# Gate and up products of a split-fp32 SwiGLU: one 512-column matmul for the weight's high part, a PSUM bank per side, product and low part on GpSimd

## The chip, the core and the metric

The kernel runs on one core of a Trainium2 chip. The time is the device time of one execution in microseconds. Beside it stands one profiled execution of the same kernel, whose trace names every instruction, its engine, its source line and its tiles. Engines are PE (TensorE), DVE (VectorE), ACT (ScalarE), POOL (GpSimd) and SP, which issues most of the DMAs.

## The reference

A two-layer decoder trunk for 256 tokens with `D_MODEL = 1024`. Each layer is a half-step SwiGLU, a token mixer and another half-step SwiGLU, each behind an RMSNorm with shift, scale and gate from the conditioning vector `c`. Layer 0 mixes with block-sparse attention (MoBA), layer 1 with MLA. All is float32. The change touches the four SwiGLUs, `D_FF = 2816`:

```python
def swiglu(h, w_gate, w_up, w_down):
    return (jax.nn.silu(h @ w_gate) * (h @ w_up)) @ w_down

for layer in range(DEPTH):
    mods = c_act @ ada_w[layer] + ada_b[layer]
    ...
    h = modulate(rms_norm(x, norm_g[layer, 0]), sh1, sc1)
    x = x + 0.5 * g1[:, None, :] * swiglu(h, ffn_w_gate[layer, 0], ffn_w_up[layer, 0], ffn_w_down[layer, 0])
    ...  # the token mixer, then the second swiglu
```

## The kernel before

**Split operands.** Every large product is made of float32r parts: a value is held as a high part (rounded) and a low part (the rest), and a product is three matmuls, high by high, high by low and low by high, summed in PSUM. `mm3` issues them (lines 394 to 396 of the profile) and then books their time on the planner's clock with `pe`. Weights come by DMA into a raw tile (`wload`); `split` makes of it `hi` on ACT and `lo` on DVE, in tiles of 128x1024, from rings of eight each (`splitp`). `in_turn` issues both, so both have line 196. `nextw` keeps one weight load ahead of the one in use.

**The activations.** `new_h` makes two tiles, `hh` and `hl`, high and low part of the transposed normalised input, each [128, 2 token blocks, 1024]. `hk_both` gives the slice of 128 features k of both token blocks, 256 columns.

**One FFN** (`ffn`) has three stages. The first 512 features of `D_FF` are made with tokens on the partitions, 512 columns a matmul. The other 2304 are made in nine blocks of 256, each two steps f of 128 features. In one step the weight is the stationary operand: for gate and then up, eight k by one `mm3` of 256 columns, 48 matmuls, all into one PSUM bank whose halves are gate and up. Then ACT makes silu of the gate half (line 560), DVE multiplies it by the up half (line 561), ACT rounds that to `gh` and DVE makes `gl`, its low part (`split_evac`, line 196). The last stage multiplies `gh` and `gl` by the down weights, 512 columns a matmul.

**Other work in the queues.** Shift, scale and gate need `c_act @ ada_w`. That is done on DVE, a multiply-add of 128x1024 for each of the 128-row pieces of `ada_w` (`ada_vec`, line 211), and the pieces are spread over an FFN by the planner: whenever its clock passes the next due time (`ada_pace`, 172 us of booked time for an FFN's pieces, 90 in the last), one piece and its DMA are issued. The first FFN also carries the bias tables for the attention (`bias_steps`, lines 722 and 785), in part on DVE, PE and POOL. Engines work off their instructions in order; the order within each is fixed when the kernel is built.

Of the kernel before, what the change touches and what calls it, by code (L numbers as in the profile page):

```python
# [10 lines left out]
F32 = mybir.dt.float32  # L11
F32R = mybir.dt.float32r
BF16 = mybir.dt.bfloat16
I32 = mybir.dt.int32
AF = mybir.ActivationFunctionType
ALU = mybir.AluOpType
# [4 lines left out]
P = 128  # L21
D = 1024
KD = D // P
S = 256
NT = S // P
# [62 lines left out]
def trunk(ctx: ExitStack, tc: tile.TileContext, a: dict, out: bass.AP):  # L88
    nc = tc.nc
# [5 lines left out]
    hp = ctx.enter_context(tc.tile_pool(name="hp", bufs=1))  # L95
# [8 lines left out]
    def nm(s):  # L104
        uid[0] += 1
        return f"{s}_{uid[0]}"
# [13 lines left out]
    def run_next():  # L120
        assert pend
        was, busy[0] = busy[0], True
        pend.pop(0)[2]()
        busy[0] = was

    def until(cond):
        while not cond():
            run_next()

    def pe(us):  # L130
        clock[0] += us
        if busy[0]:
            return
        while pend and pend[0][0] <= clock[0]:
            run_next()
        while pace[0] and clock[0] >= pace[1]:
            pace[1] += pace[0]
            ada(1)
# [54 lines left out]
    def in_turn(fn, *args, on="p", **kw):  # L193

        if started:
            return fn(*args, **kw)  # L196
        with behind(on):
            chain[on] = fn(*args, **kw)  # L198
        return chain[on]
# [94 lines left out]
    def ada(n):  # L294
        for _ in range(n):
            if next(ada_it, "end") != "end":
                ada_done[0] += 1

    def ada_pace(vectors, us):

        n = vectors * KD - ada_done[0]
        pace[0] = us / n if n > 0 else None
        pace[1] = clock[0] + (us / n if n > 0 else 0.0)
# [89 lines left out]
    def mm3(ps, lh, ll, rh, rl, start, stop):  # L393
        nc.tensor.matmul(ps, lh, rh, start=start, stop=False)  # L394
        nc.tensor.matmul(ps, lh, rl, start=False, stop=False)  # L395
        nc.tensor.matmul(ps, ll, rh, start=False, stop=stop)  # L396
        pe(3 * max(256, rh.shape[-1]) * 0.422e-3)

    def mm_tile():
        return ps_mm.tile([P, 512], F32, tag="mm", name=nm("mm"))  # L400

# [6 lines left out]
    def split_evac(hi, lo, ps):  # L408
        in_turn(nc.scalar.activation, hi, ps, AF.Copy, on="a")
        return in_turn(nc.vector.tensor_tensor, lo, ps, hi.bitcast(F32), op=ALU.subtract, on="v")  # L410
# [60 lines left out]
    pair = []  # L471

    def new_h(t):
        if t == 0:
            pair[:] = [hp.tile([P, NT, D], F32R, tag=g, name=nm(g)) for g in ("hh", "hl")]
        return pair[0][:, t, :], pair[1][:, t, :], set(), list(pair)

    def hk(h, k):
# [1 line left out]
        return kslice(h[0], k), kslice(h[1], k)  # L480

    def hk_both(h, k):
        for t in range(NT):
            until(lambda: k in h[t][2])
        return [x[:, :, k * P:(k + 1) * P] for x in h[0][3]]

    def norm_T(t, key, keep=None):
        h = new_h(t)
# [17 lines left out]
    def ffn(layer, idx, h, after, ada_to, start=None):  # L506

        last = (layer, idx) == (1, 1)
        with ExitStack() as st:
            gp = st.enter_context(tc.tile_pool(name=nm("gp"), bufs=1))  # L510
            gT = {}
            accs = start() if start else {t: [] for t in range(NT)}
            ada_pace(ada_to, 90.0 if last else FFN_PACE)
            parts = [] if start else [[], []]
            for t in range(NT):
                for i, pl in enumerate(parts):
                    ps = mm_tile()
                    for k in range(KD):
                        if len(pl) <= k:
                            pl += nextw()  # L520
                        mm3(ps, *hk(h[t], k), *pl[k], start=k == 0, stop=k == KD - 1)
                    accs[t].append(ps)
                acc = accs.pop(t)
                g = gp.tile([P, FB], F32, tag="g", name=nm("g"), bufs=2)
                nc.scalar.activation(g, acc[0], AF.Silu)
                nc.vector.tensor_tensor(g, acc[1], g, op=ALU.mult)

                def fin(t=t, g=g):
                    pt = tr_tile()
                    for j in range(FB // P):  # L530
                        nc.tensor.transpose(kslice(pt, j), kslice(g, j), ident)
                    pe(FB // P * 0.11)
                    gh, gl = [gp.tile([P, FB], F32R, tag=f"{nme}_{t}", name=nm(nme)) for nme in ("gh", "gl")]
                    split_evac(gh, gl, pt)
                    for j in range(FB // P):
                        gT[j, t] = (kslice(gh, j), kslice(gl, j))
                later(G_WAIT, fin)
            gq = gp
            for f0 in range(FB, F, S):
                if f0 == SIDE_TO * S:  # L540
                    while start and next(side[0], "end") != "end":
                        bias_step()
                    gq = st.enter_context(tc.tile_pool(name=nm("gp"), bufs=1))
                if start and f0 == ROPE_AT * S:
                    with behind("v", "a", "g"):
                        rope_tables()
                        mla_consts()
                parts = [[], []]
                for f in range(f0 // P, (f0 + S) // P):
                    ps = mm_tile().rearrange("p (i t q) -> p i t q", i=2, q=P)  # L550
                    for i, pl in enumerate(parts):
                        for k in range(KD):
                            if len(pl) <= k:
                                pl += nextw()
                            mm3(ps[:, i], *[w[:, f * P - f0:(f + 1) * P - f0] for w in pl[k]],
                                *hk_both(h, k), start=k == 0, stop=k == KD - 1)
                            if start and k in HOOKS and f0 < SIDE_TO * S:
                                bias_step()
                    g = gp.tile([P, NT, P], F32, tag="gT", name=nm("g"), bufs=2)
                    nc.scalar.activation(g, ps[:, 0], AF.Silu)  # L560
                    nc.vector.tensor_tensor(g, ps[:, 1], g, op=ALU.mult)  # L561
                    gh, gl = [gq.tile([P, NT, P], F32R, tag=f"{nme}{f}", name=nm(nme)) for nme in ("gh", "gl")]
                    split_evac(gh, gl, g)
                    for t in range(NT):
                        gT[f, t] = gh[:, t, :], gl[:, t, :]
            for half in range(2):
                acc = [mm_tile() for _ in range(NT)]
                wl = []

                def mms(t, k):  # L570
                    until(lambda: (k, t) in gT)
                    mm3(acc[t], *gT[k, t], *wl[k], start=k == 0, stop=k == KF - 1)

                lag = LAG if half == 1 else 0
                for k in range(KF):
                    if len(wl) <= k:
                        wl += nextw()
                    mms(0, k)
                    if k - lag >= 0:
                        mms(1, k - lag)  # L580
                gate = mod((layer, 2 * idx), "g")
                resid(0, half, acc[0], gate, last)
                if half == 1:
                    ada_until(ada_to)
                    after(0)
                    for k in range(KF - lag, KF):
                        mms(1, k)
                resid(1, half, acc[1], gate, last)
            after(1)
# [4 lines left out]
    def attention(ap, g, qTs, kTs, vs, bias, oT, state, after_s=None):  # L594
# [63 lines left out]
        def av():  # L658
            until(lambda: state.get("v", 0) > g)
            po = at_tile().rearrange("p (r t q) -> p r t q", r=GH // 2, t=NT)  # L660
            for pr in range(GH // 2):
                for t in range(NT):
                    for i in range(2):
                        e = 2 * pr + i
                        for kb in range(t + 1):
                            nc.tensor.matmul(po[i * DH:(i + 1) * DH, pr, t, :], vs(e, kb),  # L666
                                             pT[t, e, kb], start=kb == 0, stop=kb == t)
            pe(2.4)
            kk = g * (GH // 2)
            pov = po.rearrange("p r t q -> p t r q")  # L670
            hi, lo = [x[:, :, kk * P:(kk + 2) * P].rearrange("p t (r q) -> p t r q", q=P) for x in oT[0][3]]
            split_evac(hi, lo, pov)
            for t in range(NT):
                oT[t][2].update((kk, kk + 1))
            state["av"] = g + 1
# [609 lines left out]
```

## Time and profile before

| What | Value |
|---|---|
| median of 3 runs | 1064.85 us (1064.45 to 1068.0) |
| the profiled execution's own time | 1067.16 us |
| its span in the profile | 1065.4 us |
| busy share PE, DVE, ACT, POOL | 96%, 76%, 54%, 7% |
| mean granted TensorE clock | 0.998 |
| steps f in the gate and up stages | 72 (18 in each FFN) |
| gate and up matmuls of 256 columns | 3456 (1152 on each of lines 394, 395, 396) |

PE's busy share counts the time between a matmul's start and its modelled end, and these overlap; the pace is read from the starts. A group's row has the group's line, engine, operation, tiles and shapes, its count, then its busy time and the mean ns of one, and at last the idle time of its engine just before it with what ended that.

### The profile page before, as it was taken

The numbers are of one execution on the slowest core, as the hardware profiler recorded it, in microseconds if no ns is written. First come the engines' busy times: TensorE is split into PE (matmuls) and PEld (weight loads), VectorE is DVE, ScalarE is ACT, GpSimd is POOL, SyncE is SP. The second block draws the span as 40 slices with busy tenths as digits, with TensorE's granted clock in tenths as the row PEclk, the third lists the DMA queues.
The fourth block names the chain that finished last, engine by engine and source line by source line (L and its number), as shares of the span: only waits on it lengthen the run. The fifth ranks groups of instructions, "written<-read, shape, count | busy, mean of one in ns | idle before, by whom it ended". The sixth has DMA issues, their size and how long they took to land.

```text
span 1065.4 us, 17278 instructions
## 1 busy us (share of the span) xinstructions
PE 1020.8 (96%) x6663; PEld 899.3 (84%) x6663; DVE 810.9 (76%) x1244; ACT 578.6 (54%) x1048; POOL 70.1 (7%) x119
## 2 busy tenths in 40 slices
PE   4999999998999999999999999999988899999998
PEld 2499999886778789999887999988766778999986
DVE  5999977886875789889688888867778758755642
ACT  4364545357675765545348544533868777545531
POOL 4001000002121000000000000000043200000000
PEclk9999999999999999999999999999999999999999
DMA  9999987996845479989897997986354337665450
GB/s 311 322 304 287 376 288 278 335 318 206 310 162 170 139 236 345 337 293 332 295 313 227 328 329 251 318 303 205 117 162 142 119 119 236 223 204 187 161 177 20
DMA packets 166934, 260.65 MB, mean 245 GB/s; under 512 B 8030, under 2 KB 110214, under 8 KB 166852
## 3 DMA queue, kind: packets, MB, share of 16 engines
q1 hardware_dynamic: 164496, 254.70, 70.3%
q0 software_dynamic: 976, 3.37, 1.0%
q10 hardware_dynamic: 1380, 1.49, 0.5%
q8 instruction: 52, 0.85, 0.3%
q14 instruction: 30, 0.25, 0.1%
HBM read 255.33 MB, written 4.19 MB: 244 GB/s over the span
## 4 chain that ended last, share of the span: by engine, by line
PE 77%; DVE 10%; ACT 4%; DMA 4%; POOL 3%; issue 3%; SPq 0%; DVEq 0%; ACTq 0%; POOLq 0%
PE mm L394 23%; PE mm L396 23%; PE mm L395 23%; DVE lo L196 3%; POOL hr L703 3%; DMA adaw<-in_ada_w_dram 2%; PE mm L198 2%; ACT hi L196 1%; DVE oh L722 1%; PE adaps L222 1%; PE at L666 1%; PE at L611 1%; DVE acc L211 1%; DMA raw<-in_ffn_w_gate_dram 1%; ACT y L196 1%
## 5 line engine op out<-in xcount | busy, mean ns | idle before, releaser
L196 DVE TENSOR_TENSOR lo<-raw,hi 128x1024 fp32r<-128x1024 f32 (+2 forms) x316 | 374.3, 1199 | 80.2 <-ACT hi L196 79.3
L196 ACT ACTIVATE hi<-raw 128x1024 fp32r<-128x1024 f32 (+2 forms) x316 | 324.1, 1040 | 171.5 <-PE mm L396 103.6
L394 PE MATMUL mm<-hh,hi 128*128 128x256 f32 x1152 | 328.6, 285 | 0.0
L396 PE MATMUL mm<-hh,lo 128*128 128x256 f32 x1152 | 326.7, 284 | 0.5 <-DVE lo L196 0.5
L395 PE MATMUL mm<-hl,hi 128*128 128x256 f32 x1152 | 326.5, 283 | 0.0
L395 PEld LDWEIGHTS mm<-hl,hi 128*128 128x128 f32 x1152 | 221.7, 192 | 0.6 <-issue 0.2
L396 PEld LDWEIGHTS mm<-hh,lo 128*128 128x128 f32 x1152 | 221.6, 192 | 0.7 <-DVE lo L196 0.7
L394 PEld LDWEIGHTS mm<-hh,hi 128*128 128x128 f32 x1152 | 221.7, 192 | 0.6 <-issue 0.2
L211 DVE SCALAR_TENSOR_TENSOR acc<-adaw,cact,acc 128x1024 f32<-128x1024 f32 x126 | 162.8, 1292 | 20.6 <-DMA adaw<-in_ada_w_dram 16.2
L394 PE MATMUL mm<-hi,gh 128*128 128x512 f32 x352 | 138.0, 392 | 0.0
L395 PE MATMUL mm<-lo,gh 128*128 128x512 f32 x352 | 137.0, 389 | 0.0
L396 PE MATMUL mm<-hi,gl 128*128 128x512 f32 x352 | 137.0, 389 | 0.0
L394 PE MATMUL mm<-hi,hh 128*128 128x512 f32 (+1 forms) x240 | 96.7, 404 | 5.0 <-ACT hh L196 5.0
L396 PE MATMUL mm<-hi,hl 128*128 128x512 f32 (+1 forms) x240 | 94.0, 392 | 1.5 <-DVE hl L196 1.4
L395 PE MATMUL mm<-lo,hh 128*128 128x512 f32 (+1 forms) x240 | 93.4, 390 | 0.0
L560 ACT ACTIVATE g<-mm 128x256 f32<-128x256 f32 x72 | 27.3, 379 | 94.5 <-PE mm L396 94.5
L396 PEld LDWEIGHTS mm<-hi,gl 128*128 128x128 f32 x352 | 66.1, 188 | 13.8
L394 PEld LDWEIGHTS mm<-hi,gh 128*128 128x128 f32 x352 | 66.1, 188 | 13.2
L395 PEld LDWEIGHTS mm<-lo,gh 128*128 128x128 f32 x352 | 66.1, 188 | 13.1
L196 ACT ACTIVATE gh<-g 128x256 fp32r<-128x256 f32 x72 | 29.9, 416 | 69.6 <-DVE g L561 69.6
L394 PEld LDWEIGHTS mm<-hi,hh 128*128 128x128 f32 x240 | 45.1, 188 | 16.1 <-ACT hh L196 7.8
L396 PEld LDWEIGHTS mm<-hi,hl 128*128 128x128 f32 x240 | 45.1, 188 | 13.2 <-DVE hl L196 4.5
(222 smaller groups left out, 1114.8 us busy)
## 6 DMA issues: line engine op xcount, KB each, us to landing
adaw<-in_ada_w_dram SPq DMA_DIRECT2D x144, 512.0 KB, 6.8
raw<-in_ffn_w_gate_dram SPq DMA_DIRECT2D x42, 1024.0 KB, 7.3
raw<-in_ffn_w_up_dram SPq DMA_DIRECT2D x42, 1024.0 KB, 6.9
raw<-in_ffn_w_down_dram SPq DMA_DIRECT2D x40, 1024.0 KB, 6.6
raw<-in_moba_w_qkv_dram SPq DMA_DIRECT2D x16, 512.0 KB, 5.0
adaw<-in_kv_ada_w_dram SPq DMA_DIRECT2D x16, 512.0 KB, 5.6
raw<-in_ffn_w_down_dram SPq DMA_DIRECT2D x8, 512.0 KB, 3.6
raw<-in_moba_w_qkv_dram SPq DMA_DIRECT2D x4, 1024.0 KB
```

The source lines that it names most:

```text
L196: return fn(*args, **kw)
L198: chain[on] = fn(*args, **kw)
L211: nc.vector.scalar_tensor_tensor(acc, wt, cact[:, k:k + 1], bz if k == 0 else acc, op0=ALU.mult, op1=ALU.add)
L222: nc.tensor.transpose(kslice(pt, j), kslice(acc, 4 * hh + j), ident)
L394: nc.tensor.matmul(ps, lh, rh, start=start, stop=False)
L395: nc.tensor.matmul(ps, lh, rl, start=False, stop=False)
L396: nc.tensor.matmul(ps, ll, rh, start=False, stop=stop)
L560: nc.scalar.activation(g, ps[:, 0], AF.Silu)
L611: nc.tensor.matmul(ps3[:, i, :], qTs(e, t), kTs(e, nk), start=bias is not None, stop=bias is not None or i == len(es) - 1)
L666: nc.tensor.matmul(po[i * DH:(i + 1) * DH, pr, t, :], vs(e, kb), pT[t, e, kb], start=kb == 0, stop=kb == t)
L703: nc.gpsimd.tensor_tensor(r, v2, mhalf[:, :nh], op=ALU.pow)
L722: return fn(*args, **kw)
```

## The change

`hh` and `hl` become one tile of [128, 2 parts, 2 token blocks, 1024], and `hk_both` hands out the slice of both parts, 512 columns. `mm2` takes the place of `mm3` in the nine blocks: the weight's high part meets both parts of h in one matmul of 512 columns, whose result fills a whole bank (high by high in the first half, high by low in the second), and the weight's low part meets the high part of h in one of 256 columns, added to the second half. Gate and up have a bank each. After each side ACT copies the second half to SBUF and DVE adds the first half to it. Then ACT makes silu in SBUF, GpSimd the product, ACT `gh`, and GpSimd `gl`. A step has 32 matmuls in place of 48. The planner books 346.6 ns for an `mm2`, where it booked 324.1 ns for an `mm3`.

```diff
+    def mm2(ps, wh, wl, both, start, stop):
+        nc.tensor.matmul(ps, wh, both, start=start, stop=False)
+        nc.tensor.matmul(ps[:, 1], wl, both[:, 0], start=False, stop=stop)
+        pe(1e-3 * (6 * P / 2.4 + 2 * 13.3))
...
     def new_h(t):
         if t == 0:
-            pair[:] = [hp.tile([P, NT, D], F32R, tag=g, name=nm(g)) for g in ("hh", "hl")]
+            both = hp.tile([P, 2, NT, D], F32R, tag="hh", name=nm("hh"))
+            pair[:] = [both[:, 0], both[:, 1], both]
...
-        return [x[:, :, k * P:(k + 1) * P] for x in h[0][3]]
+        return h[0][3][2][:, :, :, k * P:(k + 1) * P]
...
                 for f in range(f0 // P, (f0 + S) // P):
-                    ps = mm_tile().rearrange("p (i t q) -> p i t q", i=2, q=P)
+                    sides = gp.tile([P, 2, NT, P], F32, tag="g", name=nm("g"), bufs=2)
                     for i, pl in enumerate(parts):
+                        ps = mm_tile().rearrange("p (i t q) -> p i t q", i=2, q=P)
                         for k in range(KD):
                             if len(pl) <= k:
                                 pl += nextw()
-                            mm3(ps[:, i], *[w[:, f * P - f0:(f + 1) * P - f0] for w in pl[k]],
-                                *hk_both(h, k), start=k == 0, stop=k == KD - 1)
+                            mm2(ps, *[w[:, f * P - f0:(f + 1) * P - f0] for w in pl[k]],
+                                hk_both(h, k), start=k == 0, stop=k == KD - 1)
...
-                    g = gp.tile([P, NT, P], F32, tag="gT", name=nm("g"), bufs=2)
-                    nc.scalar.activation(g, ps[:, 0], AF.Silu)
-                    nc.vector.tensor_tensor(g, ps[:, 1], g, op=ALU.mult)
+                        sd = sides[:, i]
+                        nc.scalar.activation(sd, ps[:, 1], AF.Copy)
+                        nc.vector.tensor_tensor(sd, ps[:, 0], sd, op=ALU.add)
+                    g = sides[:, 0]
+                    nc.scalar.activation(g, g, AF.Silu)
+                    nc.gpsimd.tensor_tensor(g, g, sides[:, 1], op=ALU.mult)
...
-                    split_evac(gh, gl, g)
+                    nc.scalar.activation(gh, g, AF.Copy)
+                    nc.gpsimd.tensor_tensor(gl, g, gh.bitcast(F32), op=ALU.subtract)
```

More of the change, by code (lines that the diff above doesn't have):

```diff
@@ L670, in av @@
             pov = po.rearrange("p r t q -> p t r q")
-            hi, lo = [x[:, :, kk * P:(kk + 2) * P].rearrange("p t (r q) -> p t r q", q=P) for x in oT[0][3]]
+            hi, lo = [x[:, :, kk * P:(kk + 2) * P].rearrange("p t (r q) -> p t r q", q=P) for x in oT[0][3][:2]]
             split_evac(hi, lo, pov)
```

## The prediction

> **What bounds the kernel now.** First I read the page's totals, then the busy time by stretch inside the four gate and up stages (the second FFN, the third, the fourth, and the end of the first). The columns are PE, PEld, DVE, ACT, POOL, granted clock, DMA share, GB/s.
>
> ```profile
> PE 1020.8 (96%) x6663; PEld 899.3 (84%) x6663; DVE 810.9 (76%) x1244; ACT 578.6 (54%) x1048; POOL 70.1 (7%) x119
> 405.00:491.00 86.00, 86.00 (x721) 86.00 (x720) 76.22 (x90) 41.40 (x59) 0.00 (x0) 1.00 0.93 319
> 597.00:681.00 84.00, 84.00 (x700) 83.83 (x700) 69.75 (x83) 39.94 (x58) 0.00 (x0) 1.00 0.87 302
> 906.00:990.00 84.00, 84.00 (x699) 83.83 (x698) 51.93 (x63) 43.20 (x62) 0.00 (x0) 1.00 0.58 193
> 117.00:165.00 48.00, 48.00 (x404) 48.00 (x403) 41.32 (x56) 24.39 (x36) 0.00 (x0) 1.00 0.94 327
> ```
>
> In these stretches PE never pauses; DVE is at 89%, 83%, 62% and 86%, ACT at about half, POOL at nothing. The chain that ended last shows one exception: from about 51 to 91 us, in the first FFN, it runs through DVE, as here.
>
> ```profile
> 51.06 1.21 DVE lo L196
> ...
> 82.16 1.27 DVE acc L211
> 83.43 1.13 DVE lo L196
> 84.56 1.57 DVE oh L722 x8
> ...
> 89.56 1.14 DVE lo L196
> ```
>
> The silus of line 560 by stretch (ACT's busy time and count) show that about four steps f fall into it:
>
> ```profile
> 50.00:75.00 25.00, 0.79 (x2) 1.00 0.91 300
> 75.00:100.00 25.00, 0.85 (x2) 0.93 0.88 287
> ```
>
> So gate and up are PE's, but for some 40 us and four steps that are DVE's, where the bias tables are made. PE's pace is read from starts of matmuls, three apart:
>
> ```profile
> 475.47 0.28 PE L394 MATMUL mm<-hh,hi 128*128 128x256 f32 x1
> 475.83 0.28 PE L394 MATMUL mm<-hh,hi 128*128 128x256 f32 x1
> 777.59 0.33 PE L394 MATMUL mm<-hi,qlT 128*128 128x384 f32 x1
> 778.11 0.33 PE L394 MATMUL mm<-hi,qlT 128*128 128x384 f32 x1
> 514.76 0.39 PE L394 MATMUL mm<-hi,gh 128*128 128x512 f32 x1
> 515.44 0.39 PE L394 MATMUL mm<-hi,gh 128*128 128x512 f32 x1
> L394 PE MATMUL mm<-hh,hi 128*128 128x256 f32 x1152 | 328.6, 285 | 0.0
> ```
>
> A matmul of 256 columns takes 0.120 us, one of 384 0.173, one of 512 0.227: a straight line, 0.107 us for 256 columns and about 13.3 ns for each matmul whatever its width. A step f of 48 matmuls takes 5.76 us, a block 11.52, the nine blocks of an FFN 103.7.
>
> How much cover DVE and ACT have is seen in the ring of split tiles. The first `lo` below ends at 385.7 and is first read by PE at 392.12, at the start of the second FFN's blocks: 6.4 us ahead. Later ACT waits for a slot that PE frees; the tile whose `lo` ends at 461.53 is first read at 475.83 (quoted above), 14.3 us ahead (tiles paired by their place in the order).
>
> ```profile
> 384.47 2.35 DVE L196 TENSOR_TENSOR lo<-raw,hi 128x1024 fp32r<-128x1024 f32 x2
> 392.12 0.28 PE L394 MATMUL mm<-hh,hi 128*128 128x256 f32 x1
> 460.30 1.23 DVE L196 TENSOR_TENSOR lo<-raw,hi 128x1024 fp32r<-128x1024 f32 x1 [0.60 <-ACT hi L196]
> 460.65 1.06 ACT L196 ACTIVATE hi<-raw 128x1024 fp32r<-128x1024 f32 x1 [0.38 <-PE mm L395]
> ```
>
> So a stage starts with about 6 us in hand: DVE or ACT may fall short by that much over 18 steps, 0.36 us a step, before PE waits.
>
> **PE, what it gains.** A pair of 512 and 256 columns takes 0.227 + 0.120 = 0.347 us in place of 0.360. There are 72 x 16 = 1152 pairs: 1152 x 13.3 ns = 15.4 us, 3.84 in each FFN; a step becomes 5.55 us. The columns streamed stay the same (768 a pair). The new matmul reads its columns in four runs of 128; the one of 256 reads two such runs and lies on the same line as the others, so I add nothing for that. [...]
>
> **DVE, what stays and what grows.** DVE loses the product and `gl` and gets two additions of the same shape, so nothing by count. The rows of the second FFN's stretch:
>
> ```profile
> L196 DVE TENSOR_TENSOR lo<-raw,hi 128x1024 fp32r<-128x1024 f32 x32 | 38.3, 1220 | 2.7 <-ACT hi L196 2.7
> L211 DVE SCALAR_TENSOR_TENSOR acc<-adaw,cact,acc 128x1024 f32<-128x1024 f32 x20 | 25.6, 1278 | 1.7 <-DMA adaw<-in_ada_w_dram 1.6
> L561 DVE TENSOR_TENSOR g<-mm,g 128x256 f32<-128x256 f32 x15 | 6.3, 419 | 2.6 <-ACT g L560 2.6
> ```
>
> The planner now books 22.5 ns more a pair, so `ada` pieces (and their DMAs on SP's queue) come earlier: 0.72 us a block more on its clock, or 0.2 piece a block where 48 are paced over 172 us; over this stretch of 7.47 blocks 1.9 us of DVE. The DMA share rises from 0.93 by the same few per cent and stays under 1.
>
> The unknown is what GpSimd does to DVE. Trace of before, while the bias tables are masked:
>
> ```profile
> 77.99 2.06 POOL L785 TENSOR_SCALAR_AFFINE_SELECT bt<-bt 128x2048 f32<-128x2048 f32 x1 [55.97 <-ACT bt L722]
> 95.04 3.23 POOL L785 TENSOR_SCALAR_AFFINE_SELECT bt<-bt 128x2048 f32<-128x2048 f32 x1 [14.99 <-DMA adaw<-in_ada_w_dram]
> 95.18 1.22 DVE L196 TENSOR_TENSOR lo<-raw,hi 128x1024 fp32r<-128x1024 f32 x1
> 96.32 3.02 DVE L211 SCALAR_TENSOR_TENSOR acc<-adaw,cact,acc 128x1024 f32<-128x1024 f32 x1
> ```
>
> The same POOL operation took 2.06 alone and 3.23 beside a DVE `lo` that ended at 96.40: it waited 1.17. The DVE multiply-add behind it took 3.02 in place of 1.28: it could start its work only at 99.34 - 1.28 = 98.06, so POOL held it for 1.66 us of its own 2.06. Whoever starts first stops the other. [...] Which DVE operations are stopped I take likewise from the rows: `lo` and `acc`, 67 of 86 us, 0.8.
>
> No row has a GpSimd operation of this shape. The nearest:
>
> ```profile
> L429 POOL TENSOR_TENSOR rstd<-var,mhalf 128x1 f32<-128x1 f32 x10 | 5.6, 556 | 585.1 <-DVE var L427 585.1
> 331.02 1.66 POOL L703 TENSOR_TENSOR hr<-hv,mhalf 128x8 f32<-128x8 f32 x1 [13.99 <-DVE hv L702]
> masks.py:199 POOL TENSOR_SCALAR_AFFINE_SELECT ident<-ident 128x128 f32<-128x128 f32 x1 | 0.3, 312 | 0.1
> ```
>
> The select grows from 0.31 us at 128 elements to 2.06 at 2048, 0.91 ns each; 256 elements of one operand would be 0.43, the low end. The two-operand power goes from 0.556 at one column to 1.66 at eight, 0.40 us fixed; 1.66 is the high end. I take 0.40 + 2 x 256 x 0.91 ns = 0.87 us, as it is an operation of two operands with a cheap function. [...] Its hold on DVE is 0.4 less, as with the select: 0.47, between 0.03 and 1.25. Four such a block, on DVE's path 0.8 of the time: 1.5 us a block.
>
> Second FFN: the 86 us are 7.47 blocks, which PE now does in 82.8. DVE needs 76.2 + 1.9 + 7.47 x 1.5 = 89.3: 6.5 short, 7.8 over nine blocks, 6.4 of it in hand. Loss 1.4. Third: 69.75 + 1.5 + 7.29 x 1.5 = 82.2 in 80.9; in hand. Fourth: no shortage. First: in the four steps that are DVE's, eight holds of 0.47 x 0.8 add 3.0 us and PE gains nothing; the other 14 steps gain 14 x 0.213 = 3.0.
>
> **ACT, which now waits more.** Its rows:
>
> ```profile
> L560 ACT ACTIVATE g<-mm 128x256 f32<-128x256 f32 x72 | 27.3, 379 | 94.5 <-PE mm L396 94.5
> L196 ACT ACTIVATE gh<-g 128x256 fp32r<-128x256 f32 x72 | 29.9, 416 | 69.6 <-DVE g L561 69.6
> ACT gh L196 <- DVE g L561: 9.1, 10, 2.8
> ACT hi L196 <- PE mm L395: 6.4, 13, 0.9
> ```
>
> A step now costs it two `hi` (2 x 1.06), two copies and a silu (3 x 0.38) and `gh` (0.42): 3.68 us. Behind the copy waits silu, for DVE's addition: 0.91 each time nothing lies between, as `gh` waits for the product now (9.1 us in 10). `gh` waits for the addition and then for POOL: 0.91 + 0.87 + about 0.8 in which POOL waits for the DVE operation that just began = 2.6. What is queued behind it is the next `hi`, and DVE's `lo` waits for that. In the built order about half of the silus and half of the `gh`s have a `hi` between: 0.45 + 1.9 on average, 6.0 us a step. PE's 5.55 plus 0.36 in hand is 5.9, so ACT costs another 0.1 x 18 = 1.8 us in each of the two FFNs where DVE is full; in the fourth the waits are shorter and cost nothing.
>
> Banks are no limit: four in the ring and one a side of 2.77 us leave 8.3 us to empty one. `gl` late is hidden, too: the down stage reads the last step's tile after 21 others.
>
> **The sum.** First FFN 0; second -3.84 + 1.4 + 1.8 = -0.6; third -3.84 + 1.8 = -2.0; fourth -3.84. Together -6.4 us: 1067.2 becomes 1060.8 for the profiled execution, which lies 2.3 over the median; on the median's scale 1058.5. About 0.3%, 3.2 us, can be told from no change.
>
> **Rivals.** *DVE becomes the bound.* If the POOL operation takes 1.3 us, its hold is 0.9, or 2.9 us a block. The second FFN is then 20 us short over its nine blocks, 6.4 of it in hand, and ends 13.9 - 3.84 = 10 later; the third, 14 short, 3.7 later; the first 5.8 - 3.0 = 2.8 later; the fourth still gains 3.84. Together +12.7, 1077.5 on the median's scale; with an operation of 1.66, by the same steps, over 1100. It decides from about 1.05 us on, where the sum is 0. For it: DVE at 89%, and the power at 1.66. Against: most of that row is the power. Chance 0.32. *ACT's waits eat the gain*: from 6.1 us a step (5.76 + 0.36) on, a stage is no faster than before; at 6.15 in the middle FFNs the sum is about 0, 1065. For it: the estimate of 6.0; against: `hi` could be put between. Chance 0.11. [...] Chance 0.04. The forecast, with everything from the full 15.4 to 3.3 gained, has 0.53.
>
> **How the numbers follow.** Full gain gives 1049, the low end. The upper end, 1082, takes in the DVE rival up to an operation of about 1.4 us. Faster is the forecast, 0.53; same the two small rivals, 0.15; slower the DVE rival, 0.32. The forecast's own range is 1049 to 1061.6.
>
> **What would show it.** Right: PE starts 0.347 us a pair; POOL operations of 0.9 when alone and up to 2.1 beside DVE; `lo` and `acc` with single ones stretched by about 0.5; the lead of `lo` over PE shrinking through the second FFN and lasting through the fourth; the fourth FFN's stage about 3.8 us shorter. Wrong: a pair at 0.360; PE waiting for `lo` or `hi` by more than a few us in all; POOL operations of over 1.1 alone.

## The result and the profile after

The changed kernel takes 1092.29 us (median of 4 runs, 1091.56 to 1094.3) against 1065.17 of the kernel before on the same chip: a ratio of 1.0253, 95% interval 1.0229 to 1.0276. It is slower by 27 us where 6 us faster was forecast, and 10 us beyond the range. The profiled execution took 1092.67 us, its span is 1090.5.

From the page of the changed kernel: the totals, the granted clock in 40 slices of 27 us, and the groups of the new tail; behind them the clock's row of the kernel before.

```profile
PE 1027.2 (94%) x5511; PEld 846.5 (78%) x5511; DVE 837.4 (77%) x1244; ACT 613.5 (56%) x1192; POOL 243.5 (22%) x263
PEclk9999999999999999989998999999899999999999
...
L402 PE MATMUL mm<-hh,hi 128*128 128x512 f32 x1152 | 412.5, 402 | 3.5 <-DVE g L571 3.5
...
L574 POOL TENSOR_TENSOR g<-g 128x256 f32<-128x256 f32 x72 | 96.9, 1345 | 367.5 <-DVE g L571 364.1
...
L576 ACT ACTIVATE gh<-g 128x256 fp32r<-128x256 f32 x72 | 30.1, 418 | 140.4 <-POOL g L574 136.3
L577 POOL TENSOR_TENSOR gl<-g,gh 128x256 fp32r<-128x256 f32 x72 | 76.1, 1056 | 39.5 <-ACT gh L576 39.5
L571 DVE TENSOR_TENSOR g<-mm,g 128x256 f32<-128x256 f32 x144 | 59.7, 415 | 31.4 <-ACT g L570 22.0
```

```profile
PEclk9999999999999999999999999999999999999999
```

Four things are seen. PE has 1152 matmuls fewer, yet its busy time rose. The clock row has three slices at 8, where before all were at 9. GpSimd's product takes 1.345 us on average. ACT waits 136.3 us for it ahead of `gh`, where before it waited 69.6 us for DVE. PE's direct wait on the new tail is only 3.5 us (bank release after an addition); so most of the 27 us is not waiting at that point.

Where, is worked out from the starts of the first and the last matmul of each FFN's nine blocks (lines 394 and 396 before, 402 and 403 after). Differences to before, in us of span:

| | nine blocks of FFN 1, 2, 3, 4 | all that lies between, from start to end | sum |
|---|---|---|---|
| after | +5.5, +4.4, -0.5, -1.9 | +17.8 | +25.2 |

The four stages that the prediction reckoned with lost 7 us; 18 us were lost where no instruction had been edited, above all from the end of the second FFN's blocks to the start of the third's (+5.4) and from the end of the third's to the start of the fourth's (+8.9).

The saving on PE itself is there, in the fourth FFN. Timeline of the changed kernel, PE:

```profile
939.84 0.28 PE L403 MATMUL mm<-hh,lo 128*128 128x256 f32 x1
939.96 0.40 PE L402 MATMUL mm<-hh,hi 128*128 128x512 f32 x1
940.19 0.28 PE L403 MATMUL mm<-hh,lo 128*128 128x256 f32 x1
...
941.60 0.28 PE L403 MATMUL mm<-hh,lo 128*128 128x256 f32 x1
```

Five pairs in 1.76 us are 0.352 us a pair; forecast 0.347, before 0.360. The 256-column matmul starts 0.23 to 0.24 us after the one of 512, not 0.227.

### The profile page after: what moved, and what is told of

Read it like the earlier page. It is cut to its first block, busy times and chain, and to the rows that moved or that the text cites. A ratio compares the mean times of both kernels' runs of the same rounds, so it can differ in the third digit from the quotient of the medians.

```text
span 1090.5 us, 15304 instructions
## 1 busy us (share of the span) xinstructions
PE 1027.2 (94%) x5511; PEld 846.5 (78%) x5511; DVE 837.4 (77%) x1244; ACT 613.5 (56%) x1192; POOL 243.5 (22%) x263
## 5 line engine op out<-in xcount | busy, mean ns | idle before, releaser
L196 DVE TENSOR_TENSOR lo<-raw,hi 128x1024 fp32r<-128x1024 f32 (+2 forms) x316 | 389.3, 1248 | 91.5 <-ACT hi L196 91.1
L402 PE MATMUL mm<-hh,hi 128*128 128x512 f32 x1152 | 412.5, 402 | 3.5 <-DVE g L571 3.5
L402 PEld LDWEIGHTS mm<-hh,hi 128*128 128x128 f32 x1152 | 217.8, 189 | 57.1 <-DVE g L571 5.3
L574 POOL TENSOR_TENSOR g<-g 128x256 f32<-128x256 f32 x72 | 96.9, 1345 | 367.5 <-DVE g L571 364.1
L211 DVE SCALAR_TENSOR_TENSOR acc<-adaw,cact,acc 128x1024 f32<-128x1024 f32 x126 | 170.4, 1353 | 8.6 <-DMA adaw<-in_ada_w_dram 7.9
L576 ACT ACTIVATE gh<-g 128x256 fp32r<-128x256 f32 x72 | 30.1, 418 | 140.4 <-POOL g L574 136.3
L394 PE MATMUL mm<-hi,hh 128*128 128x512 f32 (+1 forms) x240 | 100.1, 418 | 7.8 <-ACT hh L196 7.8
L396 PE MATMUL mm<-hi,hh 128*128 128x512 f32 (+1 forms) x240 | 96.0, 400 | 1.2 <-DVE hh L196 1.1
L577 POOL TENSOR_TENSOR gl<-g,gh 128x256 fp32r<-128x256 f32 x72 | 76.1, 1056 | 39.5 <-ACT gh L576 39.5
L571 DVE TENSOR_TENSOR g<-mm,g 128x256 f32<-128x256 f32 x144 | 59.7, 415 | 31.4 <-ACT g L570 22.0
L570 ACT ACTIVATE g<-mm 128x256 f32<-128x256 f32 x144 | 53.4, 372 | 20.8 <-PE mm L403 20.0
```

The source lines that it names most:

```text
L211: nc.vector.scalar_tensor_tensor(acc, wt, cact[:, k:k + 1], bz if k == 0 else acc, op0=ALU.mult, op1=ALU.add)
L402: nc.tensor.matmul(ps, wh, both, start=start, stop=False)
L570: nc.scalar.activation(sd, ps[:, 1], AF.Copy)
L571: nc.vector.tensor_tensor(sd, ps[:, 0], sd, op=ALU.add)
L574: nc.gpsimd.tensor_tensor(g, g, sides[:, 1], op=ALU.mult)
L576: nc.scalar.activation(gh, g, AF.Copy)
```

## Experiments

The theories at first: GpSimd's *hold* on DVE; the *chain* or queue, in which ACT's `gh`, and behind it `hi`, `lo`, the copies and the additions, wait for GpSimd; the *banks*. A later one, from the 18 us outside the stages: the *booking* of the pair on the planner's clock. Ratios are to the kernel before on the same chip, with 95% intervals; its median was 1064.5 to 1066.1 us in the four sets of runs.

**1. Product and low part on DVE.** GpSimd has no part in the tail.

```diff
-                    nc.gpsimd.tensor_tensor(g, g, sides[:, 1], op=ALU.mult)
+                    nc.vector.tensor_tensor(g, g, sides[:, 1], op=ALU.mult)
...
-                    nc.gpsimd.tensor_tensor(gl, g, gh.bitcast(F32), op=ALU.subtract)
+                    nc.vector.tensor_tensor(gl, g, gh.bitcast(F32), op=ALU.subtract)
```

> The changed kernel with product and low part on DVE in place of GpSimd; matmuls, banks, copies and additions stay. Queue theory (ACT stands at gh for GpSimd, hi and lo come late behind it, PE stalls and its clock is cut): the waits of gh fall from 136 us to about 60, and the time to 1058-1066, although DVE has two operations a step more. Hold theory (GpSimd's holds on DVE's lo and acc are the cost): the holds of 23 us go, DVE gets 60 us more work, 1065-1080. Bank and addition theory (two banks a step, the copy and addition are the cost, whoever does the rest): no gain, 1085 or more.

1083.66 us, 1.0171 [1.0131, 1.0212], in the gap between the answers of the hold and of the banks. Without GpSimd two thirds of the loss are still there.

**2. Only the tail on GpSimd.** The kernel before, its three matmuls and one bank for both sides; ACT copies the up half to SBUF, GpSimd does product and `gl`.

> The kernel before with only the tail of the change: its three matmuls a pair and one bank a step stay, ACT copies the up half to SBUF, GpSimd makes product and low part, and DVE loses both. Queue theory: gh waits for GpSimd by some 2 us a step as in the changed kernel, hi and lo come late, 1075-1090. Hold theory: DVE loses 60 us of work and gets some 20 us of holds, so 1060-1067. Bank and addition theory: the tail alone costs nothing, 1063-1067.

1070.12 us, 1.005 [1.0036, 1.0065], again none of the three answers. GpSimd's work alone, at 5 us, doesn't make the 27.

**3. `gh` on GpSimd too**, so that ACT waits for nothing there.

```diff
-                    nc.scalar.activation(gh, g, AF.Copy)
+                    nc.gpsimd.tensor_copy(gh, g)
```

> The changed kernel with the rounding copy gh on GpSimd too, so ACT never waits for GpSimd, while GpSimd has three operations a step and holds DVE more often. Queue theory: ACT's waits at gh are gone, 1058-1070. Hold theory: half as many holds again, 1095-1110. Bank and addition theory: 1085-1095.

1081.12 us, 1.0164 [1.0116, 1.0212]: 9 to 11 us better than the change (by the ratios, by the medians), though GpSimd does a third operation and the `lo` and `acc` of DVE take 14 us longer still. In its trace the group of line 402 has no idle time before it, so PE's wait for a bank is gone too. No answer fits: ACT's wait for GpSimd has a price, but is not the bulk of the 27.

**4. Product on DVE, only `gl` on GpSimd.**

> The changed kernel with the product on DVE and only the low part gl on GpSimd: ACT waits at gh for a DVE operation again, as in the kernel before, and one GpSimd operation a step of two still holds DVE. Queue theory: nearly all comes back, 1055-1066. Hold theory: half of the loss stays, 1072-1080. Bank and addition theory: 1085 or more.

1076.05 us, 1.0104 [1.0071, 1.0138]: the product's place is worth 16 us. This is in the range of the hold's answer, but by chance: what stays of the loss is the booking's, as 7 and 13 show. In this run's trace the four stages gain 3.7 us together (+1.8, -1.0, -2.6, -1.9), and the time between them loses 13.0. That is the loss that no theory so far explained, and it led to the booking: an FFN books 288 pairs x 22.5 ns = 6.5 us more, while the `ada` pieces stay paced over 172 us.

**5. The change with the old booking.**

```diff
-        pe(1e-3 * (6 * P / 2.4 + 2 * 13.3))
+        pe(3 * 256 * 0.422e-3)
```

> The changed kernel, whose pair of matmuls is booked on the planner's clock at 324.1 ns again, as the three matmuls were, in place of 346.6; nothing else differs. Booking theory: an FFN books 6.5 us more in the changed kernel (288 pairs of 22.5 ns), while the pace of 172 us for the ada pieces stays, so pieces fall past the end of gate and up and stand ahead of the next norm on DVE and on SP's queue; with the old booking the 13 to 16 us outside gate and up go, and with them most of the clock lost at the transitions after the second and third FFN: 1076 to 1080 us. Bank and GpSimd theory: the waits lie in gate and up and what follows them, the planner's order hardly matters: 1088 to 1093 us.

1075.32 us, 1.0094 [1.0065, 1.0124], the booking answer to within 1 us: 17 us back, by a number that no engine ever sees.

**6. The kernel before with the new booking.**

```diff
-        pe(3 * max(256, rh.shape[-1]) * 0.422e-3)
+        pe(3 * max(256, rh.shape[-1]) * 0.422e-3 if len(rh.shape) == 2 else 1e-3 * (6 * P / 2.4 + 2 * 13.3))
```

> The kernel before, in which only the booking of the three matmuls of gate and up is raised from 324.1 to 346.6 ns; the instructions are the same, in another order. Booking theory: the transitions after the second and third FFN get later by 4 to 8 us each, 1073 to 1080 us. Bank and GpSimd theory: without the split sides nothing waits, 1064 to 1066 us.

1081.37 us, 1.0149 [1.0104, 1.0194], the booking answer and 1 us more. The same instructions in another order cost 15 us.

**7. Product on DVE and the old booking** (4 and 5 together).

> The changed kernel with the product on DVE, only the low part on GpSimd (1076.05 us with the new booking), and the old booking of 324.1 ns. Booking theory: the 13 us outside gate and up go, the saving of 8 ns a pair stays: 1060 to 1063 us. The other theory: 1073 to 1077 us, as with the new booking.

1060.38 us, 0.9954 [0.9934, 0.9973]: faster than both kernels. Its four stages gain 1.5, 2.3, 2.6 and 2.4 us.

**8. As 7, with the 512 columns in one run**: the tile of both parts is laid out by slices of 128 features.

```diff
-            both = hp.tile([P, 2, NT, D], F32R, tag="hh", name=nm("hh"))
+            both = hp.tile([P, KD, 2, NT, P], F32R, tag="hh", name=nm("hh"))
```

> As the run with the product on DVE and the old booking, but both parts of h lie one behind the other for each slice of 128 features, so that the 512 columns of the moving operand are one contiguous run in place of four of 128. If the four runs cost time, the 512-column matmul starts its successor after 227 ns in place of 235, a pair takes 347 ns in place of 352, and the time falls by a further 4 to 6 us (1056 where the other gives 1061). If they don't, 352 stays and the times agree within 1 us.

1059.58 us, 0.9941 [0.992, 0.9962], not to be told from 7. In its timeline the 256-column matmul still starts 0.23 to 0.24 us after the one of 512, so the four runs of 128 aren't what makes the pair longer than 0.347:

```profile
899.67 0.40 PE L402 MATMUL mm<-hh,hi 128*128 128x512 f32 x1
899.91 0.28 PE L403 MATMUL mm<-hh,lo 128*128 128x256 f32 x1
```

**9. As 4 (new booking), `FFN_PACE` 178.5 in place of 172.**

> The changed kernel with the product on DVE and the new booking of 346.6 ns a pair (1076.05 us as it was), in which only FFN_PACE is raised from 172 to 178.5, by the 6.5 us that an FFN books more. If the ada pieces past the end are what the booking costs, their number by the end of the second FFN is 98 again and the time is 1058 to 1064 us. If the booking acts through the due times of other work instead, it stays at 1073 to 1077 us.

1067.6 us, 1.002 [1.0006, 1.0035]: half of the 16 us came back. Neither answer fits by itself, so pieces and due times had to be parted (13, 14).

**10. As 7, with a dummy product on GpSimd** behind DVE's; nobody reads its result.

```diff
+                    dm = gp.tile([P, NT, P], F32, tag="dm", name=nm("dm"), bufs=1)
+                    nc.gpsimd.tensor_tensor(dm, g, sides[:, 1], op=ALU.mult)
```

> The run with the product on DVE, the low part on GpSimd and the old booking (1060.4 us), with 72 further GpSimd products of 128x256 behind DVE's, whose result nobody reads. Hold theory: that GpSimd stops DVE while it works is what the product on GpSimd costs (1075.3 with it, the old booking in both): 1070 to 1076 us. Chain theory: it is that the high part on ACT, and behind it the copies, the additions and the banks, wait for GpSimd's product; nobody waits for the dummy, so 1060 to 1064 us.

1072.41 us, 1.0068 [1.0051, 1.0085]: 12 us for work that nobody waits for. So the hold is shown, and cost that much here, beside a DVE that in 7 is busy for 81.01 of 84 us of the second FFN's stage (405 to 489). It doesn't divide the 15 us between 5 and 7 into hold and chain: here DVE still makes the product itself, 31 us of work that it does not have in 5, and run 3, which takes ACT out of the chain, gained 9 to 11 though the hold grew. The two overlap, and how much of the 15 is whose stays open. The groups on DVE show the hold, first in 7, then here:

```profile
L196 DVE TENSOR_TENSOR lo<-raw,hi 128x1024 fp32r<-128x1024 f32 (+2 forms) x316 | 384.3, 1229 | 74.3 <-ACT hi L196 73.6
...
L211 DVE SCALAR_TENSOR_TENSOR acc<-adaw,cact,acc 128x1024 f32<-128x1024 f32 x126 | 165.0, 1309 | 6.8 <-DMA adaw<-in_ada_w_dram 5.5
```

```profile
L196 DVE TENSOR_TENSOR lo<-raw,hi 128x1024 fp32r<-128x1024 f32 (+2 forms) x316 | 397.8, 1273 | 67.4 <-ACT hi L196 66.8
...
L211 DVE SCALAR_TENSOR_TENSOR acc<-adaw,cact,acc 128x1024 f32<-128x1024 f32 x126 | 168.4, 1337 | 6.2 <-DMA adaw<-in_ada_w_dram 5.3
```

The same `lo` and `acc` take 13.5 and 3.4 us longer, 17 in all, 0.23 for each dummy.

**11. As 1 (all on DVE), with the old booking.**

> The changed kernel with product and low part on DVE (1083.66 us with the new booking) and the old booking; GpSimd has no part. If a low part on GpSimd is no more than a hold on DVE, this gives 1056 to 1060 us, as fast as the run with it on GpSimd or faster. If DVE is full in the first two FFNs, which gets 30 us more, it gives 1065 to 1072 us.

1065.33 us, 0.9997 [0.998, 1.0014]: 18 us better than 1 by the booking, and 5 behind 7. `gl` on GpSimd holds DVE as well, but takes 72 operations off it: in the profile of this run `lo` and `acc` have 374.6 and 163.0 us, 11.7 less than in 7, and DVE's own `gl` 30.3.

**12. As 5, with five banks for matmul tiles and three for transposes.**

```diff
-    ps_mm = ctx.enter_context(tc.tile_pool(name="ps_mm", bufs=4, space=PSUM))
-    ps_tr = ctx.enter_context(tc.tile_pool(name="ps_tr", bufs=4, space=PSUM))
+    ps_mm = ctx.enter_context(tc.tile_pool(name="ps_mm", bufs=5, space=PSUM))
+    ps_tr = ctx.enter_context(tc.tile_pool(name="ps_tr", bufs=3, space=PSUM))
```

> The changed kernel with the old booking (1075.3 us), with five PSUM banks in the ring of the matmul tiles in place of four, and three in place of four for the transposes. If the ring is the limit in gate and up, the 6.7 us in which PE waits there for DVE's addition go and it gives 1066 to 1070 us. If the waits only move to the next thing that is late (the high part, lo), it stays at 1073 to 1077 us; the ring of three could cost some us in the attention stages.

1072.87 us, 1.0061 [1.004, 1.0081]. The group of line 402, first with four banks, then with five:

```profile
L402 PE MATMUL mm<-hh,hi 128*128 128x512 f32 x1152 | 411.6, 401 | 6.8 <-DVE g L571 6.7
```

```profile
L402 PE MATMUL mm<-hh,hi 128*128 128x512 f32 x1152 | 411.7, 401 | 0.2
```

The 6.7 us of waiting for a bank are gone, the time falls by 2.4, with overlapping intervals, to just under the second answer. In the traces the four stages are 5.2 us shorter than in 5, and the stretch from the first FFN's blocks to the second's, with the MoBA attention, is 6.2 longer. Whether that is the ring of three or the clock, which falls there twice in this trace, was not parted; the same stretch is 4.1 longer than before in 10, with four banks in each ring. So the banks have a share in what the stages lose, and what a fifth is worth alone stays open.

**13. Two clocks.** As 4: due times by the new booking, the pace of the pieces by a second clock with the old one.

```diff
-    def pe(us):
-        clock[0] += us
+    def pe(us, us_p=None):
+        clock[0] += us
+        clock_p[0] += us if us_p is None else us_p
...
-        while pace[0] and clock[0] >= pace[1]:
+        while pace[0] and clock_p[0] >= pace[1]:
```

> The changed kernel with the product on DVE; the planner has two clocks: due times run by the new booking of 346.6 ns a pair, the pace of the ada pieces by a second clock with the old 324.1. If the booking costs by the pieces alone, this is the 1060.4 us of the old booking (1058 to 1062). If it costs by the due times, 1076 stays; if by both in halves, as the raised pace left it, 1065 to 1069 us.

1060.91 us, 0.9961 [0.9944, 0.9977]. All of the 16 us come back: the due times of the other work cost nothing here.

**14. The kernel before, `FFN_PACE` 165.5 in place of 172.**

> The kernel before, in which only FFN_PACE is cut from 172 to 165.5, so that the ada pieces come earlier by the 6.5 us an FFN that the new booking moved them, and nothing else is booked otherwise. If the pieces are the cost: 1076 to 1082 us, as with the new booking in the kernel before (1081.4). If the due times are: 1064 to 1067 us.

1080.04 us, 1.0142 [1.0111, 1.0172], as in 6. The pieces are the whole cost of the booking. Counted in the traces, DVE has done 96 pieces ahead of the last residuals of the second FFN in the kernel before and in 5, 7 and 13: twelve vectors of eight, what is due there. In the change and in 1, 3, 4, 6 and 14 it has done 98; at the third FFN 137 where 136 are due. The trace shows what that does, at the end of the second FFN. DVE in the kernel before, then here (the residual is `ry` and `x`, then the norm's `var`; `acc<-adaw,cact,bz` opens the next vector):

```profile
554.81 0.68 DVE L495 TENSOR_TENSOR ry<-mm,gate 128x512 f32<-128x512 f32 x1
555.53 0.69 DVE L496 TENSOR_TENSOR x<-x,ry 128x512 f32<-128x512 f32 x1
...
557.53 0.15 DVE L427 SCALAR_TENSOR_TENSOR var<-ssq,ssq 128x1 f32<-128x1 f32 x1
```

```profile
552.12 1.28 DVE L211 SCALAR_TENSOR_TENSOR acc<-adaw,cact,bz 128x1024 f32<-128x1024 f32 x1
...
555.46 1.28 DVE L211 SCALAR_TENSOR_TENSOR acc<-adaw,cact,acc 128x1024 f32<-128x1024 f32 x1
556.65 0.68 DVE L495 TENSOR_TENSOR ry<-mm,gate 128x512 f32<-128x512 f32 x1
...
558.39 0.69 DVE L496 TENSOR_TENSOR x<-x,ry 128x512 f32<-128x512 f32 x1
...
561.26 0.15 DVE L427 SCALAR_TENSOR_TENSOR var<-ssq,ssq 128x1 f32<-128x1 f32 x1
```

Two pieces of the next vector stand ahead of the residual. The blocks had begun 1.2 us earlier here, yet `ry` starts 1.8 us later and `var` 3.7. What PE makes of it, in the timeline and in two stretches (eighth column the granted clock):

```profile
562.64 1.64 PE L442 MATMUL tr<-ident,y 128*128 128x128 f32 x8 [2.29 <-ACT y L437]
565.45 0.79 PE L394 MATMUL mm<-hi,hh 128*128 128x512 f32 x1 [1.17 <-ACT hh L196]
```

```profile
560.75:564.16 3.41, 1.52 (x8) 0.80 (x8) 3.41 (x6) 3.06 (x8) 0.55 (x1) 1.00 0.89 292
564.16:570.99 6.83, 5.66 (x16) 4.28 (x15) 2.58 (x6) 5.42 (x16) 0.55 (x1) 0.50 0.86 293
```

A wait of 2.3 us, and then half the clock for 6.83 us: at most 3.4 us more. From the end of the second FFN's blocks to the start of the third's, this run loses 5.9 us (starts 498.42 and 591.38, before 499.65 and 586.67); from the third's to the fourth's, 7.7.

**15. As 7, `FFN_PACE` 176.**

> The changed kernel with the product on DVE, the old booking and FFN_PACE 176 in place of 172: one piece in 43 falls later in each FFN. If pieces near the end still crowd the norm, 1056 to 1060 us, below the 1060.4 with 172; if all that is left in them fits already, the same within 2 us; if a vector's end now falls into the wait for it (its gate is needed at the end of the down stage), 1063 to 1070 us.

1069.55 us, 1.0041 [1.0023, 1.006]: 9 us lost against 7, in the range of the third answer. The profiled execution, itself over the median, is 7.6 us longer than the kernel before behind the first FFN and 4.7 behind the second, again with half the clock (six steps, 20.5 us). Pieces that come late stand in the same queue: what is missing at an FFN's end is issued there at once. At the end of the first FFN one stands between the two operations of the residual, and `var` comes 63.3 us after the last start of the blocks, in 7 59.1:

```profile
234.94 0.68 DVE L504 TENSOR_TENSOR ry<-mm,gate 128x512 f32<-128x512 f32 x1
235.54 1.27 DVE L211 SCALAR_TENSOR_TENSOR acc<-adaw,cact,acc 128x1024 f32<-128x1024 f32 x1
236.74 0.69 DVE L505 TENSOR_TENSOR x<-x,ry 128x512 f32<-128x512 f32 x1
...
239.07 0.15 DVE L434 SCALAR_TENSOR_TENSOR var<-ssq,ssq 128x1 f32<-128x1 f32 x1
```

Behind the second FFN ACT waits for a weight that came late, for 4.03 us. Run 9, which has the right number of pieces (96) and got half back, has the same wait. There the DMAs of two pieces take SP's queue for 5.76 us; the gate weight behind them is issued at 548.19, in 13 at 542.76, and ACT waits for it:

```profile
541.63 5.76 SPq L209 DMA_DIRECT2D adaw<-in_ada_w_dram  x2
548.19 0.38 SPq L370 DMA_DIRECT2D raw<-in_ffn_w_gate_dram  x1
555.13 2.01 ACT L196 ACTIVATE hi<-raw 128x1024 fp32r<-128x1024 f32 x2 [4.62 <-DMA raw<-in_ffn_w_gate_dram]
```

Of the two values tried for the old booking, 172 is the better; other values were not tried.

## Why the prediction was wrong

The 27 us in three steps, by the medians and ratios to the nearest us: the pieces moved by the booking +17 (5; +16 in 4 against 7, +18 in 1 against 11, +15 in 6); the product on GpSimd +15 (5 against 7; +16 with the new booking, the change against 4); the rest of the edit -5 (7). In the trace of 7 the four stages gain 8.7 us and the whole span 9.9, more than those 5: this execution lies 3.2 us under its median, that of the kernel before 2.3 over.

**"The planner now books 22.5 ns more a pair ... over this stretch of 7.47 blocks 1.9 us of DVE."** This is the first step that failed. The 0.2 piece a block was right, and it was costed as busy time in the stage. It should have been followed to the end of the pace: up to the point where the planner makes up what is missing it books 172.8 us in the second FFN and 171.4 in the third (the kernel's own bookings: 112 products of 512 columns at 0.648 us, 288 of 256 at 0.324, and 6 to 7 for transposes and sums), for a pace of 172, which just fitted. With the new booking these are 180.1 and 179.2, and the planner goes on to the next vector ahead of the norm, where PE has nothing else to do (the wait of 2.29 us in 14). Priced at 2 us of cover, it cost 15 to 18. No rival was on it.

Without it the forecast would still have failed, by the second step: what holds and waits take from the stages. Run 5, with the old booking, is 9 us slower than the kernel before. Its stages are +5.3, +1.9, -1.4 and -1.9 us, where the forecast has 0, -0.6, -2.0 and -3.8; the terms follow.

**"1152 x 13.3 ns = 15.4 us."** Mechanism right, size off by a third: a pair is 0.352 us. Busy time by stretch in the fourth FFN, for the change and for run 7:

```profile
930.00:1014.00 84.00, 84.00 (x476) 72.78 (x475) 53.33 (x63) 52.68 (x92) 28.13 (x30) 1.00 0.60 201
```

```profile
898.00:982.00 84.00, 84.00 (x478) 72.97 (x477) 60.15 (x81) 54.06 (x94) 19.69 (x15) 1.00 0.60 197
```

239 pairs in 84 us are 0.3515 us (7), 238 are 0.3529; the 699 matmuls before were 233 threes, 0.3605. So 9.0 ns a pair in 7, 10.4 us in all, of which its four stages show 8.7. The line through 0.120, 0.173 and 0.227 was read from matmuls that follow their like; behind one of 512 columns the one of 256 comes 0.235 after it.

**"0.40 + 2 x 256 x 0.91 ns = 0.87 us", "its hold on DVE is 0.47".** The size was nearly right: in the changed kernel the operation takes 0.72 to 0.75 us in 51 of the 144 records of product and `gl` (0.74 at 464.34 below), while the 43 products that began beside a running `lo` or `acc` took 1.58 or more (1.71 at 462.10). DVE was held less than forecast: `lo` and `acc` grew by 22.6 us in all (389.3 + 170.4 against 374.3 + 162.8), not by 36 blocks x 1.5 = 54. The additions were not held: 405 to 426 ns in all 144 records of the changed kernel, 415 on average, 418 for the product before. But the hold cost more: 12 us for one operation a step (run 10), where 4.4 us were forecast for two. The cover of "6.4 us in hand" did not show: the second FFN's stage gains 2.3 us in 7 and loses 3.0 with the dummy, whose 18 holds there are some 4 us of DVE, an estimate from the 0.23 each. The DVE rival had the right mechanism in part, and at 1077.5 a price near run 5 (1075.3). That it came so near is luck: its operation of 1.3 us alone was not found (1.345 is the mean with GpSimd's own waiting in it), and ACT's chain, which it left out, is in the 1075.3.

**"`gh` waits ... 0.45 + 1.9 on average"** was right in size: 136.3 us in 72, 1.9 us each. Its price wasn't 1.8 us in each of two FFNs: taking ACT out of that wait (3) is worth 9 to 11.

**"Banks are no limit".** Wrong as said; here is the chain in the changed kernel's timeline:

```profile
461.61 0.42 DVE L571 TENSOR_TENSOR g<-mm,g 128x256 f32<-128x256 f32 x1
...
461.94 1.28 DVE L211 SCALAR_TENSOR_TENSOR acc<-adaw,cact,acc 128x1024 f32<-128x1024 f32 x1
...
462.10 1.71 POOL L574 TENSOR_TENSOR g<-g 128x256 f32<-128x256 f32 x1 [2.79 <-DVE g L571]
...
463.84 0.42 ACT L576 ACTIVATE gh<-g 128x256 fp32r<-128x256 f32 x1 [3.02 <-POOL g L574]
...
464.17 1.04 ACT L196 ACTIVATE hi<-raw 128x1024 fp32r<-128x1024 f32 x1
464.34 0.74 POOL L577 TENSOR_TENSOR gl<-g,gh 128x256 fp32r<-128x256 f32 x1 [0.53 <-ACT gh L576]
...
465.24 1.23 DVE L196 TENSOR_TENSOR lo<-raw,hi 128x1024 fp32r<-128x1024 f32 x1 [2.03 <-ACT hi L196]
...
466.38 0.42 DVE L571 TENSOR_TENSOR g<-mm,g 128x256 f32<-128x256 f32 x1
...
466.86 0.50 PE L402 MATMUL mm<-hh,hi 128*128 128x512 f32 x1 [1.73 <-DVE g L571]
```

DVE's `acc` stretches GpSimd's product to 1.71; `gh` waits for that 3.02, `hi` stands behind `gh`, `lo` behind `hi`, the addition behind `lo`, and PE waits 1.73 for the bank that the addition frees. The 8.3 us to empty a bank held only while nothing in that row was late.

## What to carry over

A planner's cost is part of the schedule: whoever changes a booked duration must go through every constant that was set against the sum of them (here a pace of 172 us against some 172 booked), follow what falls past it, and ask who stands in the queue behind it at the next point where PE runs dry. Test it alone, as a change of one number in the kernel before; that tells it from the edit within one run. And work given to GpSimd wasn't free of DVE here: with 256-element operations beside a DVE that in the changed kernel is busy for 92%, 89%, 88% and 63% of stretches of the four stages (120 to 165, 411 to 497, 612 to 696 and 930 to 1014 us), the product cost 15 us, by the hold and by ACT's wait for it, while `gl`, for which no engine waits in the trace of 7, gained 5.

## What was not expected of the hardware

**The clock fell after half-idle stretches of 3.41 us.** The half-clock stretches of the changed kernel start at 92.67, 249.68, 375.97, 468.13, 577.36, 778.75 and 809.47 us: all lie on one grid of 3.413 us (157.01 us between the first two are 46 of them), and last one or two steps of it. Three steps of that grid, each with what followed:

```profile
372.56:375.97 3.41, 1.64 (x8) 0.80 (x8) 3.27 (x5) 3.18 (x9) 0.19 (x1) 1.00 0.77 259
375.97:379.38 3.41, 3.22 (x8) 2.54 (x9) 1.02 (x4) 3.20 (x10) 0.56 (x1) 0.50 0.15 50
573.95:577.36 3.41, 1.31 (x6) 0.75 (x4) 3.41 (x5) 3.15 (x6) 0.55 (x1) 1.00 1.01 360
577.36:584.19 6.83, 5.97 (x18) 4.44 (x19) 3.69 (x7) 6.83 (x20) 0.55 (x1) 0.50 1.05 362
840.19:843.60 3.41, 1.90 (x13) 1.53 (x12) 3.41 (x8) 1.70 (x3) 0.00 (x0) 1.00 0.40 61
843.60:847.01 3.41, 3.10 (x20) 2.64 (x19) 3.36 (x10) 3.41 (x17) 0.00 (x0) 1.00 0.64 247
```

On the grids of before, of the change and of runs 7 and 14, between 20 and 1050 us, every full-clock step with PE busy for 1.87 us or less was followed by half the clock, and none with 1.90 or more. That is no sharp bound, as two steps each of 11 and 12 show, the first fallen at 2.29, the other not at 1.78:

```profile
89.28:92.69 3.41, 2.29 (x35) 1.75 (x31) 3.41 (x12) 2.61 (x14) 0.00 (x0) 1.00 0.84 255
92.69:96.10 3.41, 3.41 (x12) 2.83 (x12) 3.41 (x5) 0.79 (x4) 2.92 (x1) 0.50 0.97 346
180.33:183.75 3.42, 1.78 (x9) 1.18 (x8) 2.67 (x4) 1.16 (x4) 0.96 (x1) 1.00 0.95 352
183.75:187.16 3.41, 3.41 (x21) 2.91 (x20) 1.16 (x2) 2.15 (x3) 1.48 (x2) 1.00 0.84 317
```

In the step ahead of each fall PE was still busy for about half of it in the changed kernel (1.14 to 1.78 us), and in 11 a fall came behind a step with as little as 1.1 us without a matmul. In all 34.1 us ran at half the clock in the changed kernel (seven stretches, three of them of 6.83; the one at the very end left out), against 3.41 before: at most 15.4 us more of its 27, and part of how a late piece of 1.28 us comes to cost several. It is not a cause by itself: it is gone in run 5, but for one stretch at the place where the kernel before has one too (93.42 and 92.82 us).
